# Block attention of the second mixer: fp32 products replaced by split fp32r products of 256 columns, outputs summed transposed in one bank

## The chip, the cores and the metric

One core of one Trainium2 chip runs the whole program. The metric is device time in microseconds from start to end of one execution. The engines are TensorE (PE, whose weight loads the profile lists apart as PEld), VectorE (DVE), ScalarE (ACT), GpSimd (POOL) and SyncE (SP, which issues the DMAs). Each engine executes its own instructions in program order; waits between engines go through semaphores.

## The reference, cut to what matters

The program is a stack of feed forward parts and token mixers over 256 tokens of width 1024, all in float32. The second kind of mixer occurs twice (two layers) and adds three attention branches. The one that is changed:

```python
def nsa_attention(q, k_cmp, v_cmp, k_sel, v_sel, k_win, v_win, gate_logits, ...):
    # q: 8 heads of 64, in 2 groups of 4; keys and values: one head of 64 for each group
    qg = apply_rope(rms_norm_2(q, q_norm), cos, sin).reshape(B, S, G, hpg, d)
    k_sel = apply_rope(rms_norm_2(k_sel, k_norm[1]), cos, sin)
    k_win = apply_rope(rms_norm_2(k_win, k_norm[2]), cos, sin)
    gates = jax.nn.sigmoid(gate_logits).reshape(B, S, G, hpg, 3)
    ...
    o_cmp = softmax(q k_cmp / 8, blocks that ended) v_cmp       # 15 compressed blocks
    o_sel = softmax(q k_sel / 8, chosen blocks of 64, causal) v_sel
    o_win = softmax(q k_win / 8, last 512 keys, causal) v_win
    return g[..., 0:1] * o_cmp + g[..., 1:2] * o_sel + g[..., 2:3] * o_win
```

With 256 tokens there are four blocks of 64 and up to 16 may be chosen, so the selected and the window branch are both plain causal attention, over different keys and values. The result (256 x 512) goes through `w_br_b`, is gated and added to the other two branches.

## The kernel before, in words

Tokens stand in two blocks of 128 (t = 0, 1). Every dense product `x @ w` is made of three fp32r matmuls (`mm3`, lines 213 to 215): both operands are split into a part `hi`, rounded to fp32r, and the rest `lo`, and hi*hi, hi*lo and lo*hi are summed in a PSUM bank. ACT makes `hi` (line 198), DVE makes `lo` (line 200).

The attention products are plain fp32 matmuls. The profile shows each as two MATMUL records with a weight load each. For the block attention (section name `nsa`) `nqT` holds the queries transposed, with group 0 on partitions 0 to 63 and group 1 on 64 to 127, and `kT` the keys of the two branches likewise; so a product q k uses 64 rows of the array. `softmax_banks` takes a bank of 512 scores (4 heads x 128 keys at t = 0, 2 heads x 256 keys at t = 1): a mask matmul (line 462), then one matmul for each head and block of keys (line 475); then max, exp with sum, reciprocal. `prob_T` transposes the probabilities with PE (line 441) and copies them out of PSUM on ACT or DVE in turn. `pv` multiplies them with 64 columns of values (line 505), token-major. Each of the two branches and each t has a bank of its own (`po`), which DVE scales by gate / sum and adds to `ob` (lines 1062 to 1065). The compressed branch (lines 1009 to 1036) uses `kcT`, which is zero outside of a group's rows, and `vcW`.

A layer has 96 / 2 = 48 products at line 475 and as many at line 505, 48 transposes of probabilities, and 12 banks of scores. Around them, in the order that the scheduler of the tile framework writes for each engine when the program is built, stand the dense products of the gates (`mm_gate`, 96 matmuls of 512 columns for each of three branches), which PE can do while softmax runs elsewhere. Ahead of `nsa` come the sections `sb` (stick breaking), `ckv` (keys, values), `cmp` (compression), `nq` (queries) and `dsa` (sparse attention); after it `gate` transposes and splits the three outputs (`split_T`, line 245), `br` multiplies them with the branch weights.

Of the kernel before, what the change touches and what calls it, by code (L numbers as in the profile page):

```python
# [8 lines left out]
F32 = mybir.dt.float32  # L9
F32R = mybir.dt.float32r  # L10
# [6 lines left out]
P = 128  # L17
S = 256
# [12 lines left out]
# ---------------------------------------------------------------- constants that depend on shapes only  # L31
# [85 lines left out]
class K:  # L117
# [67 lines left out]
    # ------------------------------------------------------------ weights  # L185
    def load(self, w, r0, nk, c0, n, pool=None):
        """rows r0.. (nk tiles of 128), cols c0..c0+n, split exactly into hi + lo."""
        nc = self.nc
        raw = self.tile(self.wpool, [P, nk, n], "raw", bufs=RAW)
        nc.sync.dma_start(out=raw, in_=w[r0:r0 + nk * P, c0:c0 + n].rearrange("(k p) n -> p k n", p=P))  # L190
# [26 lines left out]
    def dense(self, ps, xs, w, c0, n, skew=False):  # L217
        """ps[t] = x[t] @ w[:, c0:c0 + n]; with skew token block 0 goes ahead of token block 1."""
# [26 lines left out]
    def split_T(self, src, hi, lo, k0=0, bank=None):  # L245
        """transpose 512 columns of src (f32, token-major) into hi/lo[:, k0:k0+4]."""
# [8 lines left out]
    def prenorm(self, t, g):  # L255
        """transposed x*g (hi, lo) and the per-token 1/rms."""
# [15 lines left out]
    def first_norms(self, gd):  # L272
        """prenorm() of both token blocks, the gain put on after the transposes."""
# [32 lines left out]
    def prenorms(self, gd):  # L306
        """transposed inputs of a part; the part before has left them, but for the very first."""
# [5 lines left out]
    def finish(self, t, ps, weight, post):  # L313
        """x[t] += weight * (rmsnorm(f) * post, or f)."""
# [22 lines left out]
    # ------------------------------------------------------------ feed forward  # L337
# [59 lines left out]
    def rope(self, x, cos, sin, half):  # L397
        """x: [P, G, >=2*half] in place; cos, sin: [P, 2*half], sin with its sign."""
# [10 lines left out]
    def head_rs(self, sq, n):  # L409
        """1 / rms of the last axis, from the squares [P, G, n]: exp and ln, then a step of Newton's."""  # L410
# [14 lines left out]
    def head_norm(self, out, x, s, g):  # L425
        """out = rms norm of s * x over the last axis of [P, G, n], gains g; s: one scalar per token."""
# [10 lines left out]
    def transposes(self, srcs, dst):  # L437
        """PE transposes of [P, 128] pieces into one bank, then dst [P, len, 128]."""
# [73 lines left out]
    # ------------------------------------------------------------ mixer of the first block  # L512
    def mixer1(self, nxt):
# [5 lines left out]
        with tc.tile_pool(name="mix1", bufs=1) as mp:  # L519
# [73 lines left out]
            # forget gates: -8 * cumsum(log_sigmoid(.)) with heads on partitions, in three parts of bf16  # L593
            # whose sum it is (partitions 0, 32, 64)
# [76 lines left out]
    def out_proj(self, w, order, lhs, weight, post, nxt, more=None):  # L671
        """x[t] += weight * (lhs @ w, normed or not); the last K tiles finish token block 0 first."""
# [26 lines left out]
    # ------------------------------------------------------------ mixer of the second block  # L699
    def mixer2(self, l, nxt):  # L700
# [7 lines left out]
        with ExitStack() as outer:  # L708
# [8 lines left out]
            # small vectors  # L717
# [32 lines left out]
            # ---- indexer  # L750
# [15 lines left out]
            # ---- sparse attention's q, k, v and the gates of the compressed-block attention  # L766
# [426 lines left out]
```

## Time and profile before

| | |
|---|---|
| device time, median of 3 runs | 1811.75 us (1810.66 to 1812.93) |
| profiled execution: span | 1813.0 us |
| PE busy | 99% of the span, 8875 MATMUL records |
| DVE, ACT, POOL busy | 60%, 49%, 1% |
| DMA | 305 MB, 168 GB/s |
| TensorE clock granted, mean | 0.993 |

The span is that of one profiled execution, and nothing lies around it: it is the time of that execution, 1.25 us above the median of the timed runs. A busy PE says only that some matmul was under way; what PE takes is read from the distance between the starts of matmuls that follow each other.

### The profile page before, as it was taken

Reading aid. Unit: us, or ns where it says so; the run is one execution under the profiler, and the core shown is the slowest. Engines: PE = TensorE matmul, PEld = TensorE weight load, DVE = VectorE, ACT = ScalarE, POOL = GpSimd, SP = SyncE. Lnnn points to the kernel's source line nnn. Section 1 sums busy time; section 2 is a strip of 40 time slices with the busy share of each in tenths; the row PEclk is TensorE's granted clock in tenths of the full one; section 3 lists DMA queues with packets and bytes.
Section 4 is the critical chain, followed back from the end, with each engine's and each line's share of the span. In section 5 each row is a group of like instructions: output and inputs, shape, how many; then the busy total and the mean of one; then the engine's idle time right before and its main releaser. Section 6 shows DMA issues by size and latency. Waiting matters only on the chain.

```text
span 1813.0 us, 23411 instructions
## 1 busy us (share of the span) xinstructions
PE 1790.0 (99%) x8875; PEld 1471.7 (81%) x8883; DVE 1079.1 (60%) x1705; ACT 895.2 (49%) x1358; POOL 25.9 (1%) x42
## 2 busy tenths in 40 slices
PE   8999999999999999999999999999999999999999
PEld 6888787788878888787888888888887878888887
DVE  5555565555555555797567555555556975575553
ACT  5444455444445444475555444444444755554442
POOL 0000100000000000000000000000000000000000
PEclk9999999999999999999999999999999999999999
DMA  8665644266556655544255665666555442546653
GB/s 271 185 185 184 189 134 147 83 205 180 183 186 187 185 177 183 155 141 127 71 174 176 207 186 177 201 180 182 178 185 156 140 129 70 174 163 207 181 181 128
DMA packets 154594, 305.11 MB, mean 168 GB/s; under 512 B 13641, under 2 KB 44945, under 8 KB 154481
## 3 DMA queue, kind: packets, MB, share of 16 engines
q1 hardware_dynamic: 154464, 303.61, 54.6%
q8 instruction: 70, 1.15, 0.3%
q14 instruction: 44, 0.35, 0.1%
q10 hardware_dynamic: 16, 0.00, 0.0%
HBM read 302.53 MB, written 1.05 MB: 167 GB/s over the span
## 4 chain that ended last, share of the span: by engine, by line
PE 93%; DVE 3%; DMA 2%; ACT 1%; issue 1%; SPq 0%; POOL 0%; POOLq 0%; ACTq 0%
PE mm_ffn L215 10%; PE mm_ffn L214 10%; PE mm_ffn L213 10%; PE at_ffn L215 10%; PE at_ffn L214 10%; PE at_ffn L213 10%; PE mm_gate L214 3%; PE mm_gate L215 2%; PE mm_gate L213 2%; PE at_nsa L475 1%; PE mm_m L214 1%; PE mm_m L213 1%; PE mm_m L215 1%; PE po_nsa L505 1%; PE tp_ffn L251 1%; PE po_ffn L251 1%
## 5 line engine op out<-in xcount | busy, mean ns | idle before, releaser
L200 DVE TENSOR_TENSOR lo_ffn<-raw_ffn,hi_ffn 128x1024 fp32r<-128x1024 f32 x396 | 482.8, 1224 | 477.9 <-ACT hi_ffn L198 477.2
L198 ACT CAST hi_ffn<-raw_ffn 128x1024 fp32r<-128x1024 f32 x396 | 413.3, 1048 | 523.5 <-PE at_ffn L215 337.8
L213 PE MATMUL mm_ffn<-hi_ffn,xh_ffn 128*128 128x512 f32 (+1 forms) x288 | 109.3, 379 | 2.0 <-ACT xh_ffn L292 1.1
L213 PE MATMUL at_ffn<-hi_ffn,xh_ffn 128*128 128x512 f32 (+1 forms) x288 | 109.0, 379 | 0.0
L215 PE MATMUL mm_ffn<-hi_ffn,xl_ffn 128*128 128x512 f32 (+1 forms) x288 | 108.8, 378 | 0.0
L214 PE MATMUL mm_ffn<-lo_ffn,xh_ffn 128*128 128x512 f32 (+1 forms) x288 | 108.8, 378 | 0.0
L215 PE MATMUL at_ffn<-hi_ffn,xl_ffn 128*128 128x512 f32 (+1 forms) x288 | 107.8, 374 | 0.0
L214 PE MATMUL at_ffn<-lo_ffn,xh_ffn 128*128 128x512 f32 (+1 forms) x288 | 107.7, 374 | 0.0
L215 PE MATMUL mm_ffn<-hi_ffn,al_ffn 128*128 128x512 f32 x264 | 104.5, 396 | 0.0
L215 PE MATMUL at_ffn<-hi_ffn,al_ffn 128*128 128x512 f32 x264 | 104.1, 394 | 0.0
L214 PE MATMUL at_ffn<-lo_ffn,ah_ffn 128*128 128x512 f32 x264 | 104.0, 394 | 0.0
L213 PE MATMUL mm_ffn<-hi_ffn,ah_ffn 128*128 128x512 f32 x264 | 103.8, 393 | 0.0
L214 PE MATMUL mm_ffn<-lo_ffn,ah_ffn 128*128 128x512 f32 x264 | 103.5, 392 | 0.0
L213 PE MATMUL at_ffn<-hi_ffn,ah_ffn 128*128 128x512 f32 x264 | 103.5, 392 | 0.0
L200 DVE TENSOR_TENSOR lo_gate<-raw_gate,hi_gate 128x1024 fp32r<-128x1024 f32 x48 | 58.5, 1218 | 36.2 <-ACT hi_gate L198 36.2
L214 PE MATMUL mm_gate<-lo_gate,xh_ffn 128*128 128x512 f32 x192 | 77.4, 403 | 0.6 <-DVE lo_gate L200 0.6
L213 PE MATMUL mm_gate<-hi_gate,xh_ffn 128*128 128x512 f32 x192 | 77.1, 402 | 0.0
L215 PE MATMUL mm_gate<-hi_gate,xl_ffn 128*128 128x512 f32 x192 | 76.8, 402 | 0.0
L213 PE MATMUL at_ffn<-hi_ffn,xh_wo 128*128 128x512 f32 (+1 forms) x192 | 72.7, 379 | 0.0
L214 PE MATMUL mm_ffn<-lo_ffn,xh_wo 128*128 128x512 f32 (+1 forms) x192 | 72.0, 375 | 0.0
L215 PE MATMUL mm_ffn<-hi_ffn,xl_wo 128*128 128x512 f32 (+1 forms) x192 | 71.9, 375 | 0.0
L215 PE MATMUL at_ffn<-hi_ffn,xl_wo 128*128 128x512 f32 (+1 forms) x192 | 71.8, 374 | 0.0
(562 smaller groups left out, 3965.6 us busy)
## 6 DMA issues: line engine op xcount, KB each, us to landing
raw_ffn<-in_ffn_w_gu_dram SPq DMA_DIRECT2D x176, 512.0 KB, 3.7
raw_ffn<-in_ffn_w_down_dram SPq DMA_DIRECT2D x132, 512.0 KB, 3.4
raw_gate<-in_w_gate_dram SPq DMA_DIRECT2D x48, 512.0 KB, 3.7
raw_ffn<-in_ffn_w_gate_dram SPq DMA_DIRECT2D x44, 512.0 KB, 3.9
raw_ffn<-in_ffn_w_up_dram SPq DMA_DIRECT2D x44, 512.0 KB, 3.8
raw_m<-in_w_in_dram SPq DMA_DIRECT2D x22, 512.0 KB, 4.1
raw_wo<-in_w_out_dram SPq DMA_DIRECT2D x16, 512.0 KB, 3.5
raw_sb<-in_w_in_dram SPq DMA_DIRECT2D x12, 512.0 KB, 4.5
```

Source lines behind the costliest of these rows:

```text
L198: nc.scalar.copy(hi, raw)
L200: nc.vector.tensor_sub(lo, raw, hi.bitcast(F32))
L213: nc.tensor.matmul(out, xh, wh, start=first, stop=False)
L214: nc.tensor.matmul(out, xh, wl, start=False, stop=False)
L215: nc.tensor.matmul(out, xl, wh, start=False, stop=last)
L251: nc.tensor.transpose(p[:, i], src[:, i * P:(i + 1) * P], self.ident)
L475: nc.tensor.matmul(sc[:, i, c], q, k[:, c], start=False, stop=i == len(heads) - 1 and b in (t, None))
L505: self.nc.tensor.matmul(out, PT[:, i * (t + 1) + b], v(b), start=b == 0, stop=b == t)
```

## The change

Queries: `qS[:, head]` holds the rounded part of q on the rows of the head's group and the rest of q on the other 64 rows. Keys: `kh[:, g]` holds the rounded part of group g's key on both halves, `kl` the rest. One fp32r matmul over 128 rows (q_hi k_hi + q_lo k_hi) and one over 64 rows (q_hi k_lo), each of 256 columns, replace the fp32 products; the 256 columns are two branches x 128 keys at t = 0, two blocks of keys at t = 1. The probabilities are scaled by gate / sum ahead of the transposes and split after them; the values are the stationary operand, padded with 64 zero columns so that a group's output stands on its own partitions, and all branches of a t are summed in one bank, transposed. That bank, split, is the operand of the `w_br_b` product, whose rows are loaded in another order, by two DMAs a tile.

```diff
 def load(...):
+        if isinstance(r0, list):
+            p0 = 0
+            for r, m in r0:
+                nc.sync.dma_start(out=raw[p0:p0 + m, 0], in_=w[r:r + m, c0:c0 + n])
+                p0 += m
...
-            kT = T([P, 2, S], "kT")
-            vS = [T([P, 2, P], f"vS{t}") for t in range(2)]
+            kh = T([P, 2, 2, S], "sT", 1, F32R)
+            kl = T([P, 2, S], "kT", 1, F32R)
+            vh = [T([P, 2, 3, 64], f"vh{t}", 1, F32R) for t in range(2)]
+            vl = [T([P, 2, 3, 64], f"vl{t}", 1, F32R) for t in range(2)]
...
-                self.transposes([k.rearrange("p g d -> p (g d)")], kT[:, br:br + 1, toks[t]])
+                nc.tensor.transpose(p, k.rearrange("p g d -> p (g d)"), self.ident)
+                for g in range(2):
+                    own, other = half[g], half[1 - g]
+                    nc.scalar.copy(kh[own, g, br, toks[t]], p[own])
+                    nc.scalar.copy(kh[other, g, br, toks[t]], p[own])
+                    nc.vector.tensor_sub(kl[own, br, toks[t]], p[own], kh[own, g, br, toks[t]].bitcast(F32))
+            def v_evac(t, ps, br):
+                self.scaled(hi, src, xs[t][2])
+                nc.vector.scalar_tensor_tensor(out=lo, in0=src, scalar=xs[t][2], in1=hi.bitcast(F32), ...)
...
-                self.transposes([tok[:, j]... for j in range(4)], nqT[:, :, toks[t]])
+                for g in range(2):
+                    dst = qS[:, 4 * g:4 * g + 4, toks[t]]
+                    nc.scalar.copy(dst[own], p[own])
+                    nc.vector.tensor_sub(dst[other], p[own], dst[own].bitcast(F32))
...
-                    nc.tensor.matmul(sc[:, 32 * j:32 * j + 32], nqT[:, j, toks[t]], kcT, start=False, stop=j == 3)
+                    for g in range(2):
+                        nc.tensor.matmul(sc[:, j, g], qS[:, 4 * g + j, toks[t]].bitcast(F32), kcT[:, 16 * g:16 * g + 16], ...)
...
-                nc.tensor.matmul(po..., pcT[:, 0], vcW..., start=True, stop=True)
+                for j in range(4):
+                    nc.tensor.matmul(po[:, j], vcW[:, j]..., pcT[:, 0], start=j == 0, stop=False)
+            def unit(t, g, j0, br, po, gt, last):
+                for i in range(2):
+                    nc.tensor.matmul(sc[:, i], q, hi, start=t == 1 and i == 0, stop=False)
+                    nc.tensor.matmul(sc[:, i], q[half[g]], lo, start=False, stop=t == 0 and i == 1)
...
+                nc.vector.tensor_mul(pw, pw, rd[:, :, None].to_broadcast([P, n, w]))
+                for i in range(2):
+                    for x in range(2):
+                        nc.tensor.transpose(p[:, x, i], pt[:, 2 * i + x], self.ident)
+                nc.scalar.copy(ph, p)
+                nc.vector.tensor_sub(pl, p, ph.bitcast(F32))
...
+                    for x in range(2):
+                        nc.tensor.matmul(out, wh, ph[:, x], start=False, stop=False)
+                        nc.tensor.matmul(out, wl, ph[:, x], start=False, stop=False)
+                        nc.tensor.matmul(out, wh, pl[:, x], start=False, stop=last and x == 1)
...
+                todo = [(g, j0, br) for g in range(2) for j0 in (0, 2) for br in ([None] if t == 0 else [0, 1])]
+                nc.scalar.copy(obT[t][0], po)
+                nc.vector.tensor_sub(obT[t][1], po, obT[t][0].bitcast(F32))
...
+                if o is None:
+                    oTs.append(obT)
+                    continue
```

The first place is on PE, in the first layer at t = 1, where the scores of a bank are made. `at_nsa` is a bank of scores, `cb` the constants with the mask, `tp_nsa` a bank of transposes, `P_nsa` probabilities. Before:

```order
L462 LDWEIGHTS cb
L462 MATMUL at_nsa_7394<-cb 128x2x128
L475 MATMUL at_nsa_7394<-kT_ckv_6594,nqT_nq_7002 128x128 x3
L441 MATMUL tp_nsa_7382<-ident,P_nsa_7358 128x128
L475 MATMUL at_nsa_7394<-kT_ckv_6594,nqT_nq_7002 128x128
L441 MATMUL tp_nsa_7382<-ident,P_nsa_7358 128x128
L505 MATMUL po_nsa_7388<-vS_ckv_6595,PT_nsa_7365 128x64 x2
```

With the change (line 1091 is the matmul over 128 rows, 1092 that over 64, `kh` stands in the tile `sT_ckv`, `kl` in `kT_ckv`):

```order
L1091 MATMUL at_nsa_7473<-sT_ckv_6594,qS_nq_7034 128x256
L1092 MATMUL at_nsa_7473<-kT_ckv_6595,qS_nq_7034 128x256
L1119 MATMUL tp_nsa_7385<-ident,P_nsa_7375 128x128 x4
L1091 MATMUL at_nsa_7473<-sT_ckv_6594,qS_nq_7034 128x256
L1092 MATMUL at_nsa_7473<-kT_ckv_6595,qS_nq_7034 128x256
L1079 LDWEIGHTS cb
L1079 MATMUL at_nsa_7473<-cb 128x2x128
```

Matmuls over 64 rows stood in runs; now each stands alone between matmuls over 128 rows. In both layers PE enters line 475 at 32 places before, and line 1092 at 48 places now.

The second place is on PE too, where probabilities meet values (`PT_nsa` before, `cop_nsa` and `sp_nsa` now hold them; `po_nsa` is the output bank). Before:

```order
L462 LDWEIGHTS cb
L462 MATMUL at_nsa_7396<-cb 128x2x128
L475 MATMUL at_nsa_7396<-kT_ckv_6594,nqT_nq_7002 128x128 x4
L505 MATMUL po_nsa_7388<-vS_ckv_6595,PT_nsa_7381 128x64
L441 MATMUL tp_nsa_7424<-ident,P_nsa_7410 128x128 x2
L505 MATMUL po_nsa_7388<-vS_ckv_6595,PT_nsa_7381 128x64 x2
```

With the change:

```order
L1091 MATMUL at_nsa_7698<-sT_ckv_6594,qS_nq_7034 128x256
L1131 MATMUL po_nsa_7443<-cop_nsa_7622,vh_ckv_6596 128x256
L1132 MATMUL po_nsa_7443<-cop_nsa_7622,vl_ckv_6598 128x256
L1092 MATMUL at_nsa_7698<-kT_ckv_6595,qS_nq_7034 128x256
L1079 LDWEIGHTS cb
L1079 MATMUL at_nsa_7698<-cb 128x2x128
```

A bank's probabilities took four products of 64 columns (eight records); they now take six of 256 columns, each with other weights than the one ahead of it, and the scheduler puts them between the scores of another bank. Ahead of the first `nsa` row stand 82 gate matmuls of 512 columns in the first layer, 58 before; by the last `nsa` row 171 are done, 96 before.

The third place is on DVE in `ckv`, where the keys leave PSUM (`tp_ckv` is their transposed bank, `gl_ckv` the input of the compression). Before:

```order
L200 TENSOR_TENSOR lo_nq_7026<-raw_nq_7023,hi_nq_7025 128x1024
L449 COPY oa_sb_6483<-po_sb_6485 128x256
L449 COPY kT_ckv_6594<-tp_ckv_6694 128x128
L901 COPY gl_ckv_6592<-tp_ckv_6698 64x4x128
L404 TENSOR_TENSOR ropeb_ckv_6723<-selk_ckv_6707,cf 128x2x8
```

With the change:

```order
L206 TENSOR_TENSOR lo_nq_7058<-raw_nq_7055,hi_nq_7057 128x1024
L455 COPY oa_sb_6483<-po_sb_6485 128x256
L909 TENSOR_TENSOR kT_ckv_6595<-tp_ckv_6701,sT_ckv_6594 64x128
L927 COPY gl_ckv_6592<-tp_ckv_6711 64x4x128
```

A copy that fell to DVE every second time became two subtractions each time, one for each group (the other stands right behind the last row shown); each waits for a copy of ACT's.

## Rows read from the trace of the kernel before

**Rows 1.** The page, part 1: span; busy time, share and instructions of PE.

```profile
span 1813.0 us, 23411 instructions
PE 1790.0 (99%) x8875; PEld 1471.7 (81%) x8883; DVE 1079.1 (60%) x1705; ACT 895.2 (49%) x1358; POOL 25.9 (1%) x42
```

**Rows 2.** Critical chain, 842 to 892 us: share of these 50 us by line.

```profile
by line: PE at_nsa L475 26.2%; PE po_nsa L505 21.8%; PE tp_nsa L441 14.1%; PE mm_gate L213 7.4%; PE mm_gate L215 7.2%; PE mm_gate L214 7.1%; PE po_nsa L1032 4.2%; PE po_dsa L505 3.6%; PE at_nsa L1015 3.5%; PE at_nsa L462 3.0%; PE tp_dsa L44
```

**Rows 3.** Waits of PE, 725 to 960 us: us, times, longest.

```profile
PE tp_pn L735 <- DMA pe_pn<-in_nsa_cmp_pe_dram: 3.1, 1, 3.1
```

**Rows 4.** Windows of the first layer: length, busy time by engine, granted clock, DMA.

```profile
765.00:785.00 20.00, 19.63 (x115) 16.45 (x113) 19.65 (x63) 13.70 (x24) 0.00 (x0) 1.00 0.41 122
785.00:843.00 58.00, 57.69 (x325) 46.35 (x324) 52.70 (x162) 40.21 (x91) 1.19 (x4) 1.00 0.53 156
843.00:892.00 49.00, 48.95 (x339) 39.91 (x339) 28.06 (x76) 25.55 (x86) 0.00 (x0) 1.00 0.14 43
```

**Rows 5.** Timeline of PE in `nsa`: start, us, line, operation, out<-in, form, count.

```profile
842.90 0.22 PE L1013 MATMUL at_nsa<-cb 128*128 128x128 bf16 x1
842.96 1.03 PE L1015 MATMUL at_nsa<-kcT_cmp,nqT_nq 128*128 128x32 f32 x8
843.82 0.47 PE L214 MATMUL mm_gate<-lo_gate,xh_ffn 128*128 128x512 f32 x1
...
849.51 0.38 PE L462 MATMUL at_nsa<-cb 128*128 128x512 bf16 x1
849.82 1.16 PE L475 MATMUL at_nsa<-kT_ckv,nqT_nq 64*128 64x128 f32 x8
850.90 1.13 PE L1032 MATMUL po_nsa<-vcW_cmp,pcT_nsa 128*128 128x512 f32 x2
851.87 0.27 PE L441 MATMUL tp_nsa<-ident,pc_nsa 128*128 128x128 f32 x1
851.98 0.38 PE L462 MATMUL at_nsa<-cb 128*128 128x512 bf16 x1
...
855.66 0.48 PE L475 MATMUL at_nsa<-kT_ckv,nqT_nq 64*128 64x128 f32 x2
856.08 0.33 PE L441 MATMUL tp_nsa<-ident,P_nsa 128*128 128x128 f32 x1
...
859.21 1.10 PE L505 MATMUL po_nsa<-vS_ckv,PT_nsa 128*128 128x64 f32 x8
860.12 0.47 PE L214 MATMUL mm_gate<-lo_gate,xh_ffn 128*128 128x512 f32 x1
```

**Rows 6.** Timeline of PE, 772 to 774 us: fp32r matmuls of 256 columns.

```profile
772.52 0.28 PE L213 MATMUL mm_sb<-hi_sb,xh_ffn 128*128 128x256 f32 x1
...
773.72 0.28 PE L214 MATMUL mm_sb<-lo_sb,xh_ffn 128*128 128x256 f32 x1
```

**Rows 7.** Timeline of PE in the first mixer: 96 rows and 64 rows in turn.

```profile
297.11 0.48 PE L475 MATMUL at_m<-kT_m,qT_m 64*128 64x128 f32 x2
...
297.68 0.48 PE L475 MATMUL at_m<-kT_m,qT_m 64*128 64x128 f32 x2
```

**Rows 8.** Windows behind rows 9 and behind rows 7, columns as in rows 4.

```profile
217.55:224.38 6.83, 6.13 (x14) 4.79 (x15) 4.76 (x8) 2.70 (x4) 0.00 (x0) 0.50 0.77 223
299.47:306.30 6.83, 6.83 (x19) 5.06 (x19) 3.83 (x7) 3.23 (x16) 0.00 (x0) 0.50 0.75 227
```

**Rows 9.** Timeline of PE in the first mixer: idle time before a matmul, releaser.

```profile
218.25 0.79 PE L214 MATMUL mm_m<-lo_m,xh_ffn 128*128 128x512 f32 x1 [2.66 <-DVE lo_m L200]
```

**Rows 10.** DVE by line, 785 to 843 us: busy us, mean ns, idle before.

```profile
L200 DVE TENSOR_TENSOR lo_gate<-raw_gate,hi_gate 128x1024 fp32r<-128x1024 f32 x8 | 9.7, 1209 | 0.0
L432 DVE SCALAR_TENSOR_TENSOR selk_ckv<-mm_ckv,rs_ffn,gS_pn 128x128 f32<-128x128 f32 x4 | 1.4, 346 | 0.2 <-ACT junk_ckv L430 0.2
```

**Rows 11.** Tiles `po_nsa` and `tp_nsa`: durations, ns, min/median/max.

```profile
L1064 DVE TENSOR_TENSOR rl_nsa<-po_nsa,rdb_nsa x8: 679/692/692, 860.4 to 1526.7; 128x512 f32<-128x512 f32 x8
...
L447 ACT COPY PT_nsa<-tp_nsa x12: 586/586/587, 857.4 to 1525.0; 128x512 f32<-128x512 f32 x12
```

More of the change, by code (lines that the diff above doesn't have):

```diff
@@ L930, in mixer2 @@
             kcT = T([P, 32], "kcT")
-            vcW = T([P, 8, 64], "vcW")
+            vcW = T([P, 4, 2, 64], "vcW")
             for v in range(2):
@@ L983, in nq_evac @@
                 self.rope(q, *cs(t, 16), 8)
-                self.transposes([tok[:, j].rearrange("p g d -> p (g d)") for j in range(4)], nqT[:, :, toks[t]])
+                p = self.tp([P, 4, P])
+                for j in range(4):
+                    self.lastT = nc.tensor.transpose(p[:, j], tok[:, j].rearrange("p g d -> p (g d)"), self.ident).ins
+                for g in range(2):
+                    own, other = half[g], half[1 - g]
+                    dst = qS[:, 4 * g:4 * g + 4, toks[t]]
+                    nc.scalar.copy(dst[own], p[own])
+                    nc.vector.tensor_sub(dst[other], p[own], dst[own].bitcast(F32))
             self.proj(xs, w, 768, 512, nq_evac)
@@ L999, in mixer2 @@
                     nc.vector.reciprocal(rd[:, heads[0]:heads[-1] + 1:2], den)
-                    PT = self.prob_T(lp, t, pt, "c", 2)
+                    PT = self.tile(lp, [P, 2 * (t + 1), P], "rl", bufs=2)
+                    self.transposes([pt[:, i, b * P:(b + 1) * P] for i in range(2) for b in range(t + 1)], PT)
                     for i, h in enumerate(heads):
@@ L1006, in mixer2, with compressed @@
             self.sec = "nsa"
-            ob = []
-            for t in range(2):
-                gt = gate[t].rearrange("p (h b) -> p h b", b=3)
-                sc = self.at((P, P))
+            obT = [[L([P, 4, P], f"ob{n}{t}", 1, F32R) for n in "hl"] for t in range(2)]
+            pend = []
+            def compressed(t, po, gt):
+                sc = self.at((P, 4, 2, 16))
                 with tc.issue_after(after):
-                    nc.tensor.matmul(sc, cb["identb"], cb["cmask"][:, toks[t]], start=True, stop=False)
+                    nc.tensor.matmul(sc.rearrange("p j g k -> p (j g k)"), cb["identb"], cb["cmask"][:, toks[t]],
+                                     start=True, stop=False)
                 for j in range(4):
-                    nc.tensor.matmul(sc[:, 32 * j:32 * j + 32], nqT[:, j, toks[t]], kcT, start=False, stop=j == 3)
-                s3 = sc.rearrange("p (h k) -> p h k", k=16)
+                    for g in range(2):
+                        nc.tensor.matmul(sc[:, j, g], qS[:, 4 * g + j, toks[t]].bitcast(F32),
+                                         kcT[:, 16 * g:16 * g + 16], start=False, stop=j == 3 and g == 1)
+                s3 = sc.rearrange("p j g k -> p (j g) k")
                 mx = self.sm(8, "mx")
@@ L1032, in mixer2 @@
-                nc.tensor.matmul(po.rearrange("p h d -> p (h d)"), pcT[:, 0], vcW.rearrange("p h d -> p (h d)"),
-                                 start=True, stop=True)
-                o = L([P, 8, 64], f"ob{t}")
-                nc.vector.tensor_mul(o, po, rd8[:, :, None].to_broadcast([P, 8, 64]))
-                ob.append(o)
-            pend = []
+                for j in range(4):
+                    nc.tensor.matmul(po[:, j], vcW[:, j].rearrange("p g d -> p (g d)"), pcT[:, 0],
+                                     start=j == 0, stop=False)
@@ L1067, in mixer2 @@
-            self.run(pend)
+                po = self.po((P, 4, P))
+                compressed(t, po, gt)
+                todo = [(g, j0, br) for g in range(2) for j0 in (0, 2) for br in ([None] if t == 0 else [0, 1])]
+                for k, (g, j0, br) in enumerate(todo):
+                    unit(t, g, j0, br, po, gt, k == len(todo) - 1)
+                self.run(pend)
+                nc.scalar.copy(obT[t][0], po)
+                nc.vector.tensor_sub(obT[t][1], po, obT[t][0].bitcast(F32))
@@ L1100, in mixer2 @@
                 acc = self.accs()
-                ws = [self.load(G("w_br_" + name), k * P, 1, 0, D) for k in range(nk)]
+                if o is None:
+                    ws = [self.load(G("w_br_b"), [(64 * k, 64), (256 + 64 * k, 64)], 1, 0, D) for k in range(nk)]
+                else:
+                    ws = [self.load(G("w_br_" + name), k * P, 1, 0, D) for k in range(nk)]
                 for t in range(2):
```

107 lines of the change are left out of this document (67 added, 40 removed).

## The prediction

> **What bounds the kernel now.** The page comes first [rows 1]: PE is busy 99% of a span of 1813.0 us, DVE 60%, ACT 49%. A busy PE is only one whose matmuls overlap, so I looked next for its waits in the first layer's mixer: one of 3.1 us for a small load at its start [rows 3] is the longest, and nothing comes near it. In the block attention PE waits for nobody, because the gates' matmuls, which need nothing of the attention, fill every pause of softmax. The windows [rows 4] say the same: PE full from 785 to 892 us, the clock granted at 1.00, DMA at 14% to 53%. So time here is the sum of what PE's instructions take from start to start, and a change is worth what it takes off that sum, unless another engine begins to hold PE up. The nearest to that is DVE: 52.7 of 58 us from 785 to 843 us, 19.65 of 20 us just ahead.
>
> The chain of 842 to 892 us [rows 2] gives the shares: of 50 us, scores (L475) 26.2% or 13.1 us, values (L505) 21.8% or 10.9 us, compressed branch L1032 2.1 us and L1015 1.75 us. The second layer is the same program.
>
> **The prices of PE.** All are distances between starts. An fp32 record of 128 rows takes 0.11 us whatever its columns up to 128: eight with 64 columns 859.21 to 860.12, eight with 32 columns 842.96 to 843.82, a transpose 851.87 to 851.98 [rows 5]. An fp32r matmul of 256 columns, each with new weights as here, takes 0.12 us: ten from 772.52 to 773.72 [rows 6].
>
> The price that decides is that of going from 128 rows of the array to 64 and back. Two records over 64 rows alone take 0.42 us (855.66 to 856.08), eight take 1.08 us (849.82 to 850.90), so a further record costs 0.11 us and 0.20 us is a fixed part [rows 5]. The first mixer shows the whole: there one matmul of 96 rows and 128 columns (0.06 us where the rows do not change, 842.90 to 842.96 [rows 5]) and two records of 64 rows alternate every 0.57 us [rows 7]; 0.06 + 0.22 is their own, so the round trip costs 0.29 us, and 0.09 of it lies ahead of the first record.
>
> The Trainium skill, TensorEngine Tiling, section Tiling Modes (Key Properties), says that changing the tiling mode, and not only the tile, drains the engine. The trace agrees (0.29 us a round trip [rows 5, 7]); by the rule, as by the rows, the change's 24 entries a layer are paid for, and it gives no figure of its own.
>
> **The change part by part, for one layer.**
>
> Scores. Before: 13.1 us plus 16 entries x 0.09 us that the chain books on what stands ahead = 14.5 us. After: 24 pairs (12 banks x 2 heads) of a matmul over 128 rows and one over 64, so 48 x 0.12 = 5.8 us and 24 entries x 0.29 = 7.0 us: 12.8 us. Gain 1.7 us. That fp32r over 64 rows pays the same switch is not in the trace; the bounds are no switch (gain 8.7 us) and a switch of 0.40 us, with one more exposed record time of 0.11 us (loss 0.9 us). I take 0.29, since behind bf16 and behind fp32 it is alike.
>
> Values. Before 10.9 us by the chain, or 9.7 to 10.9 us at 0.10 to 0.114 us a record. After 72 matmuls x 0.12 = 8.6 us. Gain 1.1 to 2.3; I take 1.8.
>
> Compressed branch. Scores: 8 matmuls of 16 columns take the place of 4 of 32 at each t, and the cost goes by record: 16 more records x 0.11 = 1.8 us lost. Values: two records of 512 columns, 0.97 us (850.90 to 851.87 [rows 5]), become eight of 0.11: 0.2 us gained over both t. Loss 1.6.
>
> Transposes behind the attention: eight of `ob` are left out: gain 0.9.
>
> Sum: 1.7 + 1.8 - 1.6 + 0.9 = 2.8 us a layer, 5.6 us in the two layers.
>
> Work off PE. DVE: the keys take 8 subtractions of 64 x 128 for 2 copies and the values 4 new operations, at L432's 0.35 us each [rows 10] 3.5 us; the queries 4 subtractions of 512 columns for one copy, at 0.69 us [rows 11] 2.1 us; inside `nsa` 12 scalings and 12 subtractions of 0.69 us replace 6 copies, 8 operations of L1064's and L1065's kind and 2 of L1035's, net 8 x 0.69 = 5.5 us, and small ones near 1 us. ACT gets 14 more small copies in `ckv`, three of 0.59 us [rows 11] in `nq` and six in `nsa`. I cost this at nothing but 0.5 us a layer, and the cover is the gates' matmuls: in `nsa` DVE was at 28.06 of 49 us [rows 4] and rises to about 35 in a longer stretch. Ahead of it the scheduler has put 82 gate matmuls before the first `nsa` row instead of 58; these 24 take 24 x 2 x 0.12 = 5.8 us of PE and two more `lo_gate` of 1.21 us [rows 10] of DVE. So DVE needs 52.7 + 5.6 + 2.4 = 60.7 us of 63.8, 95% where it was 91%. At 98% in 765 to 785 us PE was still 19.63 of 20 us busy [rows 4].
>
> Queued behind: PE's products with the values now wait for ACT's copy (0.59 us) and DVE's subtraction (0.69 us) one after the other, where one copy did before. The order leaves at least 0.7 us of other PE work between transposes and the first product, mostly over 1 us, and the products with the rest come last; two or three units a layer may wait 0.2 us. The output bank is single, and the second block's first product must wait until the first block's sum is copied and split (1.3 us); three gate matmuls, a transpose and two scores stand between. The 0.5 us a layer is for these. The added DMA issues (four a layer on SP) and GpSimd's memsets are far ahead of their use and cost nothing; without that cover they would cost tenths.
>
> **The sum.** 1813.0 - 5.6 + 1 = 1808.4 us for the profiled execution; it stood 1.25 us above the median of the runs, so against 1811.75 us I say **1807.2 us**, 0.25% less. What can be told from no change is 0.2%, 3.6 us.
>
> **The rivals.**
>
> *The switch is not paid* by fp32r pairs. For it: only that no fp32r over 64 rows is in the trace. Against it: it showed behind bf16 and fp32 alike. Then 8.7 us a layer for the scores in place of 1.7: 1793.2 us. Chance 0.12, which includes a switch that is paid in part.
>
> *DVE becomes the bound ahead of `nsa`* (the other side). PE waits for a late `lo_gate`, as it once waited 2.66 us for `lo_m` in the first mixer [rows 9]. Behind that wait PE had 6.8 us at half the clock, 1.2 GHz for 2.4 [rows 8], which cost it 3.4 us. From 2.8 us of waits a layer the gain is gone; with one such wait and such a clock, 6.1 us a layer, the time is 1807.2 + 12.2 = 1819.4 us, with the wait alone in both layers or one whole event in one of them 1812.6 to 1813.3 us; half way, 1816 us, stands for it. For it: 95% is an average, and the subtractions wait for ACT. Against it: 98% did no harm. Chance 0.18.
>
> *The clock falls inside `nsa`.* Two to three us of 96 and 64 rows in turn [rows 7] were followed by 6.8 us at half the clock too [rows 8], without any wait. The new scores are such turns. Against it: they come in bursts of 1.1 us between dense matmuls, and only in one place three banks stand close. One fall like that costs 3.4 us of PE, two 6.8 us: 1810.6 to 1814 us, no change. Chance 0.10.
>
> *The gain is eaten in part* by short waits for softmax, 1 to 3 us a layer more than the 0.5: 1809 to 1813 us. Chance 0.12.
>
> *As forecast*, 1803 to 1810.5 us by the bounds of the values' price and of the switch: chance 0.48.
>
> **How the numbers follow.** Faster (below 1808.1): the free switch 0.12 and 0.34 of the forecast's 0.48, whose middle lies a little below that line: 0.46. Slower (above 1815.4): 0.12 of the DVE case and 0.04 for falls of the clock with waits: 0.16. The rest, 0.38, is within 0.2%. The range reaches down to half of the free switch, 1800 us, and up to the DVE case, 1816 us; the forecast's own is 1803 to 1810.5.
>
> **What would show it.** Right: in the first layer lines 1091 and 1092 alternate with starts near 0.22 and 0.31 us; runs of lines 1131 to 1133 at 0.12 us; line 1053 at 0.11 us a record; PE without a wait over 0.5 us in 785 to 900 us; clock 1.00 there. Wrong: 0.12 us from 1092 to 1091 (the switch is free), waits of PE for `lo_gate` or `sp_nsa` above 1 us, or a granted clock under 1 in `nsa`.

## The result, and the profile after

The changed kernel takes **1823.3 us** (median of 4 runs, 1820.5 to 1825.5); the kernel before took 1812.3 us beside it (1810.7 to 1814.8). The ratio is 1.0062 with a 95% interval of 1.0048 to 1.0076: 0.6% slower, 9 to 14 us, where 1807.2 us was forecast and 1816 us was the upper end of the range.

The page of the changed kernel, part 1, beside [rows 1]:

```profile
span 1818.7 us, 23354 instructions
...
PE 1789.9 (98%) x8779; PEld 1463.7 (80%) x8779; DVE 1102.3 (61%) x1769; ACT 915.3 (50%) x1408; POOL 26.0 (1%) x50
```

The span is only 5.7 us longer, because the profiled execution was the fastest of the four, and because its first mixer, which the change does not touch, had 3.1 us less up to the second mixer's first product (726.3 us instead of 729.4 us). The time of an execution stands 1.8 us above its span (1820.52 us for the span of 1818.7 us), so the span of 1813.0 us of the kernel before belongs to a time near 1814.8 us, the slowest of its four, and not to one 1.25 us above the median; the forecast is a difference of spans and does not change by it. PE is as busy as before and DVE 23 us busier. So the busy times tell nothing of where 11 us went; the places do. Windows from the first product of the keys' projection (`ckv`) to that of the queries (`nq`), from there to the first gate product, and from there to the first of `br`, first layer. The columns are those of [rows 4]. The kernel before:

```profile
777.71:801.25 23.54, 23.18 (x132) 19.18 (x134) 22.03 (x58) 17.45 (x39) 0.00 (x0) 1.00 0.50 141
801.25:817.72 16.47, 16.47 (x95) 13.66 (x93) 15.80 (x57) 11.53 (x26) 1.19 (x4) 1.00 0.51 157
817.72:937.20 119.48, 119.12 (x669) 95.45 (x669) 72.87 (x166) 69.14 (x159) 0.00 (x0) 1.00 0.40 119
```

And the changed kernel:

```profile
774.88:800.21 25.33, 23.34 (x134) 19.16 (x133) 23.84 (x67) 18.49 (x41) 0.00 (x0) 1.00 0.51 146
800.21:817.63 17.42, 16.94 (x88) 12.86 (x89) 16.06 (x56) 12.82 (x35) 1.18 (x4) 1.00 0.33 97
817.63:937.68 120.05, 119.62 (x624) 93.06 (x622) 82.13 (x191) 77.35 (x173) 0.00 (x0) 1.00 0.41 122
```

The block attention itself lies in the third window: 0.6 us more, where 2.8 us less were forecast. (0.56 us of it are four transposes of `cmp` that now stand behind the first gate product.) The two stretches ahead of it, which get keys, values and queries ready, lose 1.8 and 0.95 us, and DVE has 23.84 of 25.33 us to do there where it had 22.03 of 23.54. The waits of PE in this layer, beside [rows 3] (us in total, times, longest):

```profile
PE tp_pn L741 <- DMA pe_pn<-in_nsa_cmp_pe_dram: 3.4, 1, 3.4
PE mm_nq L219 <- DVE selk_ckv L413: 1.6, 1, 1.6
PE tp_ckv L904 <- DVE selk_ckv L413: 0.4, 2, 0.2
...
PE mm_gate L220 <- DVE lo_gate L206: 0.3, 1, 0.3
```

New are the wait of 1.6 us for the first query product and the two for `tp_ckv`, all for DVE and none in the block attention; the kernel before had that of 0.3 us for `lo_gate` too. The second layer shows the same waits, and there PE's clock falls to half (1.2 GHz) behind the longest (first row), where the kernel before had the full clock (second row):

```profile
1440.63:1444.04 3.41, 3.41 (x15) 3.18 (x15) 2.48 (x4) 1.83 (x9) 0.62 (x2) 0.50 0.35 79
1440.00:1444.00 4.00, 4.00 (x25) 3.40 (x24) 3.92 (x15) 2.51 (x8) 0.56 (x2) 1.00 0.48 135
```

The fall does not follow every such wait: in the first layer of the changed kernel, and in both layers of e1 below, the wait is the same and the clock stays at 1.00.

In the block attention the timeline of PE answers to [rows 5]:

```profile
874.70 0.66 PE L1119 MATMUL tp_nsa<-ident,P_nsa 128*128 128x128 f32 x4
875.11 0.36 PE L1091 MATMUL at_nsa<-sT_ckv,qS_nq 128*128 128x256 f32 x1
875.40 0.38 PE L1092 MATMUL at_nsa<-kT_ckv,qS_nq 64*128 64x256 f32 x1
875.72 0.28 PE L1079 MATMUL at_nsa<-cb 128*128 128x256 bf16 x1
875.75 0.36 PE L1091 MATMUL at_nsa<-sT_ckv,qS_nq 128*128 128x256 f32 x1
876.05 0.38 PE L1092 MATMUL at_nsa<-kT_ckv,qS_nq 64*128 64x256 f32 x1
876.36 0.38 PE L1091 MATMUL at_nsa<-sT_ckv,qS_nq 128*128 128x256 f32 x1
876.67 0.38 PE L1092 MATMUL at_nsa<-kT_ckv,qS_nq 64*128 64x256 f32 x1
```

From 1091 to 1092 it is 0.29 to 0.31 us, from 1092 to 1091 0.31 us (876.05, 876.36, 876.67). A pair therefore takes 0.62 us; 0.24 are its own, and 0.38 the round trip between 128 and 64 rows. Forecast were 0.22 + 0.31 = 0.53. The chain of 854 to 901 us, beside [rows 2] (a piece lasts there until the next begins to count, so it divides a pair otherwise than the starts do):

```profile
by line: PE at_nsa L1092 15.9%; PE mm_gate L219 11.4%; PE mm_gate L220 11.2%; PE mm_gate L221 11.0%; PE at_nsa L1091 10.4%; PE tp_nsa L1119 9.0%; PE po_nsa L1131 5.3%; PE at_nsa L1079 5.2%; PE po_nsa L1133 5.0%; PE po_nsa L1132 4.5%; PE po_
```

The three products with the values, forecast at 0.12 us, do take 0.12 us where they follow each other, and 0.21 us where a matmul over 64 rows follows:

```profile
866.26 0.28 PE L1133 MATMUL po_nsa<-sp_nsa,vh_ckv 128*128 128x256 f32 x1
866.38 0.28 PE L1131 MATMUL po_nsa<-cop_nsa,vh_ckv 128*128 128x256 f32 x1
866.50 0.28 PE L1132 MATMUL po_nsa<-cop_nsa,vl_ckv 128*128 128x256 f32 x1
866.62 0.28 PE L1133 MATMUL po_nsa<-sp_nsa,vh_ckv 128*128 128x256 f32 x1
866.83 0.38 PE L1092 MATMUL at_nsa<-kT_ckv,qS_nq 64*128 64x256 f32 x1
```

### The profile page after: what moved, and what is told of

It reads as the page before. It is cut to its first block, busy times and chain, and to the rows that moved or that the text cites. A ratio compares the mean times of both kernels' runs of the same rounds, so it can differ in the third digit from the quotient of the medians.

```text
span 1818.7 us, 23354 instructions
## 1 busy us (share of the span) xinstructions
PE 1789.9 (98%) x8779; PEld 1463.7 (80%) x8779; DVE 1102.3 (61%) x1769; ACT 915.3 (50%) x1408; POOL 26.0 (1%) x50
## 4 chain that ended last, share of the span: by engine, by line
PE 91%; DVE 4%; DMA 2%; ACT 1%; issue 1%; SPq 0%; POOL 0%; POOLq 0%; ACTq 0%
PE mm_ffn L221 10%; PE mm_ffn L220 10%; PE mm_ffn L219 10%; PE at_ffn L221 10%; PE at_ffn L220 10%; PE at_ffn L219 10%; PE mm_gate L220 3%; PE mm_gate L219 2%; PE mm_gate L221 2%; PE mm_m L220 1%; PE mm_m L219 1%; PE mm_m L221 1%; PE tp_ffn L257 1%; PE po_ffn L257 1%; PE at_m L481 1%; PE at_nsa L1092 1%
```

## The experiments

Two theories were set against each other. **A**: the round trips between 128 and 64 rows cost it. **B** and later **D**: late work on DVE costs it. Times are medians of the kernel; the kernel before, run beside them, stood at 1812.4 to 1813.8 us. The changed kernel itself was timed only with the result above, so an experiment is compared with it by way of the kernel before, which ran beside both: by the ratios, e1's 17.6 us below are 17.4 us, and e6's 9.8 us are 9.6 us.

**e1: no matmul over 64 rows.** 

```diff
-            kl = T([P, 2, S], "kT", 1, F32R)
+            kl = [T([P, 2, S], n, 1, F32R) for n in ("kT", "iT")]
+            for g in range(2):
+                nc.gpsimd.memset(kl[g][half[1 - g]].bitcast(F32), 0.0)
...
-                    nc.tensor.matmul(sc[:, i], q[half[g]], lo, ...)
+                    nc.tensor.matmul(sc[:, i], q, lo, ...)
```

> The product with the keys' rest is made over 128 rows instead of 64: the other 64 rows of the rest are set to zero once, so nothing else changes and no matmul of the block attention uses 64 rows any more. Theory A (the price is that of going from 128 rows to 64 and back, 0.385 us a time by the trace of the changed kernel, 24 times a layer): 48 x 0.385 = 18.5 us less, 1823.3 to about 1805 us, which is below the kernel before. Rival B (the loss comes from late work on DVE and ACT; without the switch PE would only wait longer for softmax): less than 5 us gained, 1818 to 1823 us, and PE waits appear in the block attention.

Measured: 1805.7 us, ratio to the kernel before 0.9966 (0.9953 to 0.9979). As A says, 17.6 us less than the changed kernel. The pairs now start 0.24 us apart (882.02 to 882.26):

```profile
881.81 0.37 PE L1093 MATMUL at_nsa<-sT_ckv,qS_nq 128*128 128x256 f32 x1
882.02 0.28 PE L1094 MATMUL at_nsa<-kT_ckv,qS_nq 128*128 128x256 f32 x1
882.13 0.28 PE L1093 MATMUL at_nsa<-sT_ckv,qS_nq 128*128 128x256 f32 x1
882.26 0.28 PE L1094 MATMUL at_nsa<-kT_ckv,qS_nq 128*128 128x256 f32 x1
882.38 0.28 PE L1081 MATMUL at_nsa<-cb 128*128 128x256 bf16 x1
```

The wait of 1.6 us stayed, and the two stretches ahead kept their length (25.2 and 17.4 us). All of the gain lies from the first gate product to `br`, 112.0 us instead of 120.05 in the first layer:

```profile
819.79:931.81 112.02, 111.58 (x622) 90.51 (x622) 81.61 (x191) 76.77 (x173) 0.00 (x0) 1.00 0.44 131
```

**e2 and e3: fewer and more round trips.** e2 (first diff) puts the two products over 128 rows of a bank ahead of the two over 64; e3 (second) cuts each in two of 128 columns.

```diff
                 for i in range(2):
                     q = qS[:, 4 * g + j0 + i, toks[t]]
...
                         nc.tensor.matmul(sc[:, i], q, hi, ...)
+                for i in range(2):
+                    q = qS[:, 4 * g + j0 + i, toks[t]]
                     nc.tensor.matmul(sc[:, i], q[half[g]], lo, ...)
```

```diff
-                        nc.tensor.matmul(sc[:, i], q, hi, ...)
-                    nc.tensor.matmul(sc[:, i], q[half[g]], lo, ...)
+                    for b in range(2):
+                            nc.tensor.matmul(sc[:, i, b], q, hi[:, b], ...)
+                        nc.tensor.matmul(sc[:, i, b], q[half[g]], lo[:, b], ...)
```

> Order inside a bank of scores: both products over 128 rows first, then both over 64 rows, so the 48 entries to 64 rows become 26 in both layers by the built order of PE. Theory A: 22 x 0.385 = 8.5 us less, about 1815 us. Rival B: within 2 us of the changed kernel, 1821 to 1825 us.

> Each product of 256 columns in the scores is cut in two of 128 columns and the two kinds alternate, so there are 96 entries to 64 rows in place of 48; columns and operands are the same. Theory A: 48 x 0.385 = 18.5 us more, about 1842 us. Rival B: the extra switches lie in time that PE would wait anyway, below 1830 us.

Measured: e2 1814.8 us, 8.5 us less, as A says. e3 1864.4 us, 41 us more and not 18.5. Where the clock is still full, a cut pair takes 0.51 us from start to start (863.08 to 863.59), so two take 0.40 us more than the one of 0.62 us that they replace, which is A's price:

```profile
863.08 0.33 PE L1093 MATMUL at_nsa<-kT_ckv,qS_nq 64*128 64x128 f32 x1
863.33 0.33 PE L1092 MATMUL at_nsa<-sT_ckv,qS_nq 128*128 128x128 f32 x1
863.59 0.33 PE L1093 MATMUL at_nsa<-kT_ckv,qS_nq 64*128 64x128 f32 x1
```

The windows show what came on top: within the block attention, with PE busy throughout and little or no DMA, the clock falls (a value between 0.5 and 1 is the mean of stretches at the one and at the other).

```profile
823.26:860.00 36.74, 36.31 (x189) 27.41 (x188) 30.39 (x83) 26.09 (x52) 0.00 (x0) 1.00 0.51 158
860.00:880.00 20.00, 20.00 (x93) 16.21 (x93) 10.24 (x32) 9.21 (x40) 0.00 (x0) 0.75 0.14 49
880.00:900.00 20.00, 19.92 (x98) 16.16 (x97) 10.25 (x25) 8.31 (x22) 0.00 (x0) 0.83 0.09 27
900.00:920.00 20.00, 20.00 (x80) 15.85 (x79) 10.57 (x28) 6.47 (x21) 0.00 (x0) 0.60 0.00 0
920.00:940.00 20.00, 20.00 (x96) 16.47 (x95) 9.86 (x13) 11.15 (x17) 0.00 (x0) 0.97 0.39 109
```

With 0, 26 and 48 round trips in the two layers the times are 1805.7, 1814.8 and 1823.3 us, 0.35 to 0.39 us each; at 96 the line breaks. From the first gate product (823.26 us) to `br` (967.02) e3 takes 143.8 us, 23.7 more than the changed kernel; 24 x 0.385 = 9.2 us are the round trips. The other 14.5 us go with the clock: by its means the four windows from 860 to 940 us give up at most 17 us. In the changed kernel the clock is 1.00 there, so the forecast's rival of a fall inside `nsa` was not met; e3 shows that it can be. Whether it is the round trips that bring the clock down or the cutting of the matmuls was not tried apart.

**e4 and e5: the values' rest.** In the changed kernel DVE makes it from the PSUM bank of the projection, behind stick breaking's work, and the first query product needs a free bank. The diff is e4's; e5 has `nc.gpsimd.tensor_sub` in its last line.

```diff
                 self.scaled(hi, src, xs[t][2])
-                nc.vector.scalar_tensor_tensor(out=lo, in0=src, scalar=xs[t][2], in1=hi.bitcast(F32), ...)
+                vf = I([P, 2, 64], "vf", 2)
+                self.scaled(vf, src, xs[t][2])
+                nc.vector.tensor_sub(lo, vf, hi.bitcast(F32))
```

> The rest of the values is made by DVE from a copy in SBUF that ACT writes (one more ACT operation of 0.36 us for each), instead of from the PSUM bank of the projection. Theory C (the wait of 1.6 us of PE ahead of the first product of the queries is for this bank, which DVE reads late): the wait goes in both layers, and in the second layer the half clock behind it; 3 to 5 us less, 1818 to 1820 us. Rival (what is late is DVE as a whole, and PE waits next for the transposes of the keys or for the gates' lo): less than 1.5 us.

> As the kernel in which ACT copies the values out of the bank, but GpSimd, not DVE, subtracts: four operations of 0.35 us a layer leave DVE, no switch of rows is touched. Theory D (between the projections of the keys and the first gate product DVE is full, and PE loses there about what DVE was given more, 3.7 us of new operations less 0.6 of old in a layer): about 1.4 us less a layer, 1820 to 1821 us. Rival (the order of DVE's work, not its amount): within 1 us of 1823 us, with other waits.

Measured: e4 1822.0 us (1.0048, 1.0031 to 1.0064): no gain that can be told. Theory C fell, though its mechanism is there: the wait of 1.6 us is gone, so it was for the bank, and PE waits next for other results of DVE.

```profile
PE mm_nq L220 <- DVE lo_nq L206: 1.6, 2, 1.0
PE at_cmp L974 <- DVE cop_cmp L972: 0.9, 1, 0.9
```

e5 1819.2 us (1.0036, 1.0025 to 1.0048), 4 us less than the changed kernel, as D says or a little more. The intervals of e4 and e5 overlap, and that of e5 just touches the changed kernel's, so it takes e6 to say that DVE's work counts and not where the bank is read.

**e6: the keys' subtractions left out as well, on top of e5.**

```diff
+            nc.gpsimd.memset(kl.bitcast(F32), 0.0)
...
-                    nc.vector.tensor_sub(kl[own, br, toks[t]], p[own], kh[own, g, br, toks[t]].bitcast(F32))
```

> As the one with GpSimd, and the eight subtractions for the rest of the keys (0.29 us each, 2.3 us a layer) are left out: the rest stands at zero, so the product with it adds nothing, but PE does all its matmuls. DVE then has no more to do in this stretch than in the kernel before. Theory D: PE's loss there (2.7 us in the first layer, 4.1 in the second, with the half clock behind its wait) is gone: 1816 to 1818 us. Rival: over 1820 us.

Measured: 1813.5 us (1.0009, 0.9999 to 1.0019), the time of the kernel before. What these operations take on DVE in the changed kernel, both layers (ns min/median/max):

```profile
L909 DVE TENSOR_TENSOR kT_ckv<-tp_ckv,sT_ckv x16: 282/288/295, 802.7 to 1456.6; 64x128 fp32r<-64x128 f32 x16
L915 DVE SCALAR_TENSOR_TENSOR vl_ckv<-mm_ckv,rs_ffn,vh_ckv x8: 340/348/352, 791.1 to 1448.8; 128x128 fp32r<-128x128 f32 x8
```

That is 16 x 0.288 + 8 x 0.348 = 7.4 us of DVE, and PE gained 9.8 us by their absence. The three windows of the first layer are together 159.3 us, those of the kernel before 159.5:

```profile
776.32:799.79 23.47, 23.17 (x131) 19.18 (x133) 22.27 (x58) 17.97 (x41) 1.59 (x2) 1.00 0.51 142
799.79:815.25 15.46, 15.11 (x82) 12.06 (x81) 14.25 (x50) 13.25 (x38) 2.56 (x5) 1.00 0.42 127
815.25:935.66 120.41, 119.98 (x630) 93.45 (x629) 82.91 (x193) 77.67 (x174) 0.31 (x1) 1.00 0.41 122
```

**e9 and e12: the load alone, in the kernel before.** The diff is e9's; a tag (`dm` here) names a set of buffers that its tiles take in turn. e12 has the tag `dmk` with four buffers for the first and `dmv` with two for the second.

```diff
                 self.transposes([k.rearrange("p g d -> p (g d)")], kT[:, br:br + 1, toks[t]])
+                for g in range(2):
+                    own = slice(64 * g, 64 * g + 64)
+                    dm = I([P, P], "dm", 2)
+                    nc.vector.tensor_sub(dm[own], kT[own, br, toks[t]], k[own].rearrange("p g d -> p (g d)"))
...
                 self.scaled(vS[t][:, 0], ps[:, 384:512], xs[t][2])
+                nc.vector.scalar_tensor_tensor(out=I([P, P], "dm", 2), in0=ps[:, 384:512], ...)
```

> The kernel before, with the change's DVE load alone: behind the keys' transposes eight subtractions of 64 x 128 a layer and four operations of 128 x 128 that read the values' PSUM bank once more; nobody uses what they write. Theory D (DVE is full between the keys' projection and the first gate product, so what it is given there PE loses): 12 operations of 0.2 to 0.35 us, 2.5 to 3.7 us a layer, 1818 to 1820 us. Rival (the loss of the changed kernel comes from its longer chains, ACT's copy and then DVE's subtraction, not from the load): below 1815 us.

> The kernel before with the DVE load alone, as in the earlier run of that kind, but the new results stand in two tags (four buffers for the keys' operations, two for the values') and not in one tag of two buffers; PE's built order then is that of the changed kernel between the two projections (the first query product stands ahead of the eight products of stick breaking's values). Theory D: 12 operations a layer, 3.3 us by the lengths seen in that earlier run, 2 to 3.5 us a layer lost, 1817 to 1820 us. Rival (the loss needs the chain of ACT's copy and DVE's subtraction, which is not here): below 1815 us. If it is near 1834 us again, the shared tag was not what put 10 us between the projections there.

Measured: e9 1834.2 us, 21 us more than the kernel before; e12 1822.3 us (1.0053, 1.0036 to 1.0070), 8.5 us more. In e9 the two buffers of one tag, shared by twelve results, changed PE's built order: the last 24 of the 48 products of the keys' second projection stand behind stick breaking's products and the first transposes, and nothing is left to fill stick breaking's pauses. PE waits there 1.7 us for `zs` and 1.5 us for `rl`, both of ACT and of stick breaking, and 1.7 us for the shared tag, and the clock's mean is 0.62 from 800 to 813.3 us. e12 has buffers enough, PE's order is near that of the changed kernel, and it shows the same first wait as that kernel (its profiled execution was the slowest of its six, 1828.5 us):

```profile
PE mm_nq L213 <- DVE selk_ckv L407: 1.6, 1, 1.6
PE mm_gate L213 <- DVE sm_cmp L421: 1.5, 1, 1.5
PE mm_gate L214 <- DVE lo_gate L200: 1.1, 3, 0.6
...
PE mm_nq L214 <- DVE lo_nq L200: 0.5, 1, 0.5
```

So the load alone, with no split product and no new chain from ACT to DVE, does to the kernel before what the change did: D holds. Its price is near one for one or above it: 2 x (8 x 0.287 + 4 x 0.344) = 7.4 us of DVE, and 6.5 to 12.7 us of the kernel by the interval.

One rival lies close: the load also changes the order that is built for PE. In the kernel before, seven products of the queries stand ahead of the twelve products of stick breaking's values (`po_sb`), which wait for ACT; in the changed kernel, e1 and e12 only one does, and it is the one that waits 1.6 us; in e5, e6 and e13 there are seven again. e4 speaks against this order as the whole cause: it has the full load on DVE, seven products there and no wait for the bank, and its time cannot be told from the changed kernel's. How much of the loss is DVE's time itself and how much the order built around it is not shown.

**e7 and e8: compressed scores in fp32r.** Two fp32r matmuls of 16 columns, on e1, in place of one in fp32 (two records); e8 adds the edit of e5.

```diff
-                        nc.tensor.matmul(sc[:, j, g], qS[...].bitcast(F32), kcT[:, 16 * g:16 * g + 16], ...)
+                        for n in range(2):
+                            nc.tensor.matmul(sc[:, j, g], qS[...], kcT[n][:, 16 * g:16 * g + 16], ...)
```

> On the kernel with the rest over 128 rows (1805.7 us): the scores of the compressed blocks as two fp32r matmuls of 16 columns (key rounded, key's rest) in place of one fp32 matmul of two records; as many matmul records, 32 a layer. Theory E (a record of fp32 costs 0.11 us, an fp32r one of few columns 0.06 us like the bf16 one of 128 columns): 64 x 0.05 = 3.3 us less, about 1802.5 us. Rival (any change of weights costs 0.11 us): the same, 1805 to 1806 us.

> Rest of the keys over 128 rows, compressed scores in fp32r, values split on ACT and GpSimd. By the sum of A, E and D: 1823.3 - 18.5 - 3.3 - 2.8 = 1798.7 us. Rival (DVE's order decides the last): about 1802 us.

Measured: e7 1809.0 us (0.9980, 0.9972 to 0.9989), e8 1803.8 us (0.9952, 0.9936 to 0.9968). E fell, its rival holds: sixteen fp32r matmuls of 16 columns take as long as sixteen fp32 records, 0.11 us each. Why e7 is 3 us behind e1 is not settled; its profile shows 1.4 us more before the first gate product of the first layer only, where the clock's mean is 0.76 for 4.07 us behind the same wait of 1.6 us. e8 is 5 us above its sum and nearer to its rival.

**e10, e11, e13, e14: the keys' rest on GpSimd too, and the compressed scores as one matmul a head.** The diff is e11's, on e1 and e5. e10 and e13 leave out its last four lines, which make the compressed scores; e13 and e14 have the tag `kd` in place of `vf`.

```diff
+                kf = I([P, P], "vf", 2)
+                nc.scalar.copy(kf, p)
...
-                    nc.vector.tensor_sub(kl[g][own, br, toks[t]], p[own], kh[own, g, br, toks[t]].bitcast(F32))
+                    nc.gpsimd.tensor_sub(kl[g][own, br, toks[t]], kf[own], kh[own, g, br, toks[t]].bitcast(F32))
...
+                        nc.tensor.matmul(sc[:, 2 * j + g], qS[...], kcT[:, g], ...)
+                s3 = T([P, 8, 16], "pc", 2)
+                nc.scalar.copy(s3, sc[:, :, 0])
+                nc.vector.tensor_add(s3, s3, sc[:, :, 1])
```

> Rest of the keys over 128 rows, and both rests (keys and values) subtracted by GpSimd from a copy that ACT writes, so DVE has none of the new work ahead of the queries. By theories A and D: 1805.7 less the 9.8 us that the kernel without these subtractions gained (1823.3 to 1813.5), 1796 us. Rival (GpSimd, or ACT's extra copies, become late in their turn): 1799 to 1804 us, with PE waits for them.

> As the one before, and the compressed scores as one fp32r matmul of 32 columns (the key rounded and its rest side by side) for each head, summed by ACT and DVE: 32 matmuls fewer in both layers. Theory F (each matmul with new weights of 4 bytes costs 0.11 us whatever its columns): 32 x 0.11 = 3.5 us less than that one, about 1792.5 us. Rival (the two new operations at the head of the softmax make PE wait): no gain.

> Rest of the keys over 128 rows, both rests subtracted by GpSimd; ACT's copy of the keys stands in a tag of its own (two buffers that the indexer has left), not in the two of the values. PE's built order of the two projections is again that of the kernel before. Theories A and D: 1795 to 1797 us. Rival (it was GpSimd or ACT and not the shared buffers that cost 10 us a layer in the earlier run): 1810 us or more.

> As the one before, with the compressed scores as one fp32r matmul of 32 columns for each head. The earlier pair of runs with this difference stood 2.4 us apart, 3.5 us are expected by 0.11 us for each matmul left out: 1792 to 1794 us. Rival: no gain.

Measured: e10 1815.2, e11 1812.8, e13 1804.8 (0.9951, 0.9939 to 0.9963), e14 **1797.5 us** (0.9913, 0.9900 to 0.9927). e10 and e11 repeat e9: the tag that keys and values share holds the second projection up, and the same order of PE comes out, 35.1 us from `ckv` to `nq` instead of 23.4 in e13. e13 was expected 9 us below e1 and is 1 us below it: the rival holds in part. GpSimd takes 0.5 to 0.85 us for each subtraction, ACT has one copy more, and small operations of DVE that meet GpSimd take up to 483 ns (ns min/median/max, e13):

```profile
L410 DVE TENSOR_TENSOR ropeb_ckv<-selk_ckv,cf x8: 158/164/391, 800.6 to 1444.1; 128x16 f32<-128x16 f32 x8
L412 DVE TENSOR_TENSOR ropea_ckv<-selk_ckv,cf x8: 175/184/483, 802.1 to 1444.3; 128x32 f32<-128x32 f32 x8
```

In the changed kernel the longest of the second line takes 189 ns. The Trainium skill, SBUF — State Buffer, section Who interferes with whom, says that a DVE instruction with two inputs in SBUF contends with a GpSimd instruction that reads SBUF; these two lines are of that kind, and the trace agrees: each of their operations of over 380 ns starts while a GpSimd subtraction runs and ends within 0.05 us of its end. An operation with a single input (line 424, 128 x 2) is stretched likewise, from 151 to 444 ns, which that sentence does not cover. e14 is 7.3 us below e13, more than the 3.5 us of F; in the windows of the first layer 2.5 us of it lie from the first gate product to `br` (111.9 and 109.4 us), 1.8 us by the sixteen matmuls left out. In both layers it is 4.1 us (table below), near F's 3.5; the profiled executions differ by 4.2 us, and the rest of the 7.3 us between the medians is not settled.

**e15: e14 with the keys' rest back on DVE.**

> Rest of the keys over 128 rows, compressed scores as one fp32r matmul of 32 columns for each head, and GpSimd for the values' rest alone (four operations a layer), the keys' rest on DVE as in the changed kernel. By the runs so far: 1823.3 - 17.6 (rows) - 4.1 (values) - 3.5 to 7.3 (compressed scores) = 1794 to 1798 us. Rival (the eight subtractions of the keys on DVE cost more than GpSimd's slowing of DVE): 1798 us or more, behind the run with both on GpSimd (1797.5 us).

Measured: 1801.0 us (0.9938, 0.9924 to 0.9952), 3.5 us behind e14, as the rival says, though the two intervals just overlap. What GpSimd is worth for the keys stays open all the same: e14 against e15 speaks for a gain, e13, which with e5's 4 us should lie below 1802 us and does not, for a loss. e14 has the lowest median of the study.

The windows from the first product of `ckv` to the first of `br`, both layers together, leave out the stretches that no edit touches (one profiled execution each):

| kernel | us | against the kernel before |
|---|---|---|
| before | 319.1 | |
| changed | 327.0 | +8.0 |
| e4 | 325.7 | +6.7 |
| e5 | 323.0 | +4.0 |
| e6 | 318.9 | -0.1 |
| e12 | 332.8 | +13.7 |
| e1 | 309.5 | -9.5 |
| e13 | 307.7 | -11.3 |
| e14 | 303.6 | -15.4 |
| e15 | 304.9 | -14.2 |

The changed kernel and e6 say the same here as their medians. e13, without any of the load on DVE, gains 1.8 us over e1, where D alone would give 8 to 10. The copies of ACT and the subtractions of GpSimd that took the load's place are the likely reason; they were not tried one by one. e14 and e15 lie 1.3 us apart, less than their medians do.

## Why the prediction was wrong

**The step that failed first is "Work off PE ... I cost this at nothing but 0.5 us a layer, and the cover is the gates' matmuls".** The cover is good inside `nsa`, where PE waits for nobody. But the new subtractions of keys and values are made in `ckv` and `nq`, ahead of the first gate product, where PE has little to fill a pause with and DVE had 22.0 of 23.5 and 15.8 of 16.5 us to do. That "at 98% PE was still 19.63 of 20 us busy" [rows 4] was read as slack; it only showed that the load of that time could just be borne. The two stretches cost 2.75 us in the first layer and, with the half clock behind the wait, 4.1 us in the second; e6 puts all of it at 9.8 us by the medians (8.1 us by the windows), e12 at 8.5 us in the kernel before.

**The rival "DVE becomes the bound ahead of `nsa`"** had the mechanism (chance 0.18) but the wrong place and bound: not a late `lo_gate` (0.3 us) but the first query product, 20 us earlier, and the waits behind it. Its 1816 us were set half way; with the gain gone too the time went above it. The rival of short waits for softmax was not met: PE has no wait in the block attention.

**A second step failed, the sum of PE's own gain: the price of the switch was mis-sized**: 0.29 us was taken, 0.38 us measured for fp32r pairs, near the upper bound of 0.40. So the 24 pairs take 24 x 0.62 = 14.9 us where the scores before took 14.5: the term of 1.7 us a layer is gone (with the masks, and summed from each start to the next, 15.7 us before and 15.2 now). The rival of a free switch fell. That the row pointed at the right mechanism, e1 to e3 show: 17.6 us of the changed kernel are this price.

**Values**: 72 matmuls at 0.12 us hold only where they stand together; summed from start to start they take 9.65 us in place of 8.6, against 10.2 before: a gain of 0.5 and not 1.8 us a layer. **Compressed branch**: 1.7 us lost, 1.6 forecast; e14 gets it back. **Transposes** gained more than the 0.9 us: summed likewise, those of the probabilities fell from 6.1 to 4.6 us, since four stand together. The eight transposes of `ob` that are left out were worth 0.8 us. The gates' matmuls take 1.7 us more, mostly the first of a run: behind other work it mostly costs 0.31 to 0.34 us to the next gate product instead of 0.23 (0.34 us from 867.76), and there are 26 such starts instead of 14. Together, 0.5 + 0.5 - 1.7 + 0.8 + 1.5 - 1.7 = -0.1: this part of the sum is nothing and not 2.8 us a layer. e6, with all of PE's changes and without the twelve subtractions a layer for keys and values, says the same: it takes the time of the kernel before.

**What would show it**: 1131 to 1133 at 0.12 us, right in runs; line 1053 at 0.11 us, right; no wait over 0.5 us in the block attention and clock 1.00 there, right; 1091 and 1092 at 0.22 and 0.31 us, wrong in the first (0.29 to 0.31 us); "from 785 to 900 us no wait over 0.5 us", wrong at 800.2 us.

In numbers: 1807.2 us, less the 1 us allowed for stalls, plus 5.6 us of gain that was not there, plus 8.5 to 9.8 us for DVE, is 1820.3 to 1821.6 us; measured were 1823.3. The last 1.7 to 3.0 us are about the half width of the interval (2.5 us) and are not explained further.

## What to carry to other kernels

Cover must be asked for at the place where the work is done: in the stretch where DVE already had 22.0 of 23.5 us to do, 7.4 us more in the two layers came back as 8 to 10 us of the bound engine, whatever fills that engine's pauses later. Moving such work to other engines need not give it back (e13). Matmuls over part of the rows that alternate with full ones cost a round trip each time (0.38 us here); with zeros in the unused rows such a product took 0.12 us, and the kernel 17.6 us less. A small edit that shares a tag of two buffers between two uses can reorder a whole section; compare the built order before a time is read as the price of the edit.

## What was not expected of the hardware

With twice the round trips of the changed kernel, between matmuls cut in two, TensorE's clock fell with no wait of PE in the stretch: its mean was 0.60 of full speed in 900 to 920 us of e3, where PE was busy for 20.00 of 20 us. Which of the two did it is not shown. An fp32r matmul of 16 columns takes 0.11 us when each has new weights, no less than an fp32 record. DVE operations of 0.16 to 0.19 us take up to 0.48 us beside GpSimd.
